# Six gate projections as seven products of half blocks in a hybrid FFT and mLSTM block

## The chip, the cores and the metric

The kernel runs on one core of a Trainium2 chip. A core has TensorE (PE, matrix products), VectorE (DVE), ScalarE (ACT), GpSimdE (POOL) and SyncE (SP), which here only issues transfers; 16 DMA engines move data between DRAM and the core's memory. The metric is device time of one execution in microseconds (us), as the median of several. One more execution is recorded by the hardware profiler; the rows that are quoted come from it.

## The reference

The input is one sequence of 512 tokens with 1024 channels, all in float32. What matters here:

```python
h = rmsnorm(x, norm_w[l])
proj = h @ w_in[l]
x_f, z_f, x_m, z_m, o_m, g_logits = jnp.split(proj, split_points, axis=-1)

y_a = (fourier_mix(x_f) * jax.nn.silu(z_f)) @ w_fourier[l]

x_c = jax.nn.silu(centred_dwconv(x_m, conv_w[l], conv_b[l]))
q = block_diag_proj(x_c, w_q[l])
k = block_diag_proj(x_c, w_k[l])
v = block_diag_proj(x_m, w_v[l])
...                                   # gates i and f of both directions
h_cell = jnp.transpose(h_fwd + h_bwd, (0, 2, 1, 3))
h_cell = h_cell * jax.nn.sigmoid(o_m.astype(jnp.float32)).reshape(bsz, seq, M_HEADS, M_HEAD_DIM)
h_cell = h_cell * lax.rsqrt(jnp.mean(h_cell * h_cell, axis=-1, keepdims=True) + EPS)
h_cell = h_cell.reshape(bsz, seq, M_WIDTH).astype(x.dtype) * hnorm_w[l]
y_b = ((h_cell + skip_w[l] * x_c) * jax.nn.silu(z_m)) @ w_mlstm[l]

g_a, g_b = jnp.split(jax.nn.sigmoid(g_logits), N_BRANCHES, axis=-1)
x = x + (g_a * y_a + g_b * y_b) @ w_out[l]

return rmsnorm(x, final_norm_w)
```

The mLSTM has four heads of 512 channels. `z_m` and `o_m` are the two gates of each head: each is a product of the normalised input (512 x 1024) with 1024 x 512 weights. These gates are what the change touches.

## The kernel before

**Arithmetic.** Every float32 operand is split into a high and a low part, and a product is three matmuls: high x high, high x low, low x high (lines 97 to 99). The high part is a copy on ACT (line 90), the low part a subtraction on DVE (line 93).

**Weights.** All weights come in units of 128 x 1024 floats (512 KB), in the order of one list, `plan`. `fetch` loads a unit on SP's queue into one of three `raw` buffers; `prepare` splits it into `whi` and `wlo`, of which there are two buffers each (a stage late in the kernel, from about 490 us, has two more, `gwh` and `gwl`). `unit()` prepares ahead until two units are there and hands out the first. A unit's split can therefore begin when TensorE has finished with the unit two back. A unit holds 24 matmuls of 512 columns.

**Stages.** The first 20 units or so are projections that feed a convolution on DVE and ACT. Then come the four heads, one after the other; after them the branch's output product, the Fourier branch, the merge and the last product. These later projections and the last product are worked as blocks of 2 x 2 in seven products instead of eight, with sums of weight blocks that are formed in DRAM during the earlier stages: `sum_job` copies 1 MB on SP's queue and, one job later, adds another 1 MB to it in an accumulating transfer on POOL's queue. The table `JOBS` says before which units the jobs come, and one more is placed in each head after q and after the scores.

**One head.** q is projected (`vhi`, `vlo`), then scores `sp` = k x q per token block (TensorE), multiplied on DVE by decay weights `ws` of both directions: for each of four token blocks, 640 columns, because the diagonal block is there once per direction (lines 516 to 528). Meanwhile TensorE does o's four units (lines 557 to 559). DVE adds the weighted scores per direction (`sf`, `sb_`), TensorE sums them over partitions into `den` (line 608); ACT takes the absolute value (612), DVE the maximum (613) and the reciprocal (614), ACT spreads the result over the partitions (618, `rs`, in the tiles phi and plo). DVE multiplies `ws` by it (623 to 625), and `phi` and `plo` are its two parts. TensorE projects v (`vp`, line 636, small matmuls) and forms pv from those parts. z's four units stand around den, pv and the transposes (`z_unit`, evacuated at 367, SiLU at 369). pv is multiplied by the sigmoid of o (572, 652), POOL computes the inverse root of its mean square (`rr`, 656 and 657), DVE scales (658), TensorE transposes (668), and DVE combines skip, norm weight and z (670, 671) into u, which is split again into `sa` and `sb`.

**What sets the order.** The Tile scheduler orders each engine's instructions from dependences, buffers and its own model of durations; some are pinned to the order of the program. Each engine then works through its list in that order, and waits at the first instruction whose inputs or buffer are not ready.

Of the kernel before, what the change touches and what calls it, by code (L numbers as in the profile page):

```python
# [14 lines left out]
S = 512  # L15
# [6 lines left out]
NB = 5  # L22
JOBS = (10, 13, 16, 22, 26, 29, 34, 37, 42, 45, 51, 56, 60)
# [7 lines left out]
LOW = ("ones", "mhalf", "warm", "vecs", "raw", "whi", "wlo", "consts", "rb", "rc", "rr", "ss", "fss", "gb")  # L31
# [9 lines left out]
def hybrid_block(ctx: ExitStack, tc, xT, xn, first, units, blocks, vecs, gates, gbias, consts, dft, fnw, out):  # L41
# [430 lines left out]

    u_hi, u_lo = {}, {}
    for h in range(NH):
# [37 lines left out]
        def decay():  # L512
            ws = [tl(f"wf{b}", [P, 640]) for b in range(4)]
            for dr in range(2):
                bc = bank("acc")
                te.matmul(bc, bsel[:, 4 * dr + h : 4 * dr + h + 1].to_broadcast([P, P]), mx_r, start=True, stop=True)
                for b in range(4):
                    n = (b + 1) * P
                    o, s = (slice(n, 640), slice(b * P, S)) if dr == 0 else (slice(0, n), slice(0, n))
                    r = 32 * dr + h  # L520
                    se.activation(ws[b][:, o], bc[:, s], AF.Exp, scale=-1.0, bias=a_col[:, b, r : r + 1])
            for b in range(4):
                n = (b + 1) * P
                blk = ws[b][:, n : n + P]
# [5 lines left out]
            return ws  # L530

        if h > 0:
            ws = decay()
        sps = []
        for b in range(4):
            sp = bank("wk")
# [7 lines left out]
        else:  # L544
# [3 lines left out]
            ws = decay()  # L548
        ops = [bank("acc") for _ in range(4)]
# [16 lines left out]
        o_unit(0)  # L566
        so2 = [tl(f"so{n}", [P, 2, S]) for n in range(2)]
        so = [so2[t // 2][:, t % 2, :] for t in range(4)]

        def o_gate():  # L570
            for t in range(4):
                se.activation(so[t], ops[t], AF.Sigmoid, scale=rc[:, t : t + 1])
# [7 lines left out]
        for acc, first, rest, off in ((sf, 0, (1, 2, 3), P), (sb_, 3, (2, 1, 0), 0)):  # L580
            for b in rest:
                n = (b + 1) * P
                rng = slice(n - P, S) if off else slice(0, n)
                wr = slice(n, 640) if off else slice(0, n)
                if b == rest[0]:
                    full = slice(P, 640) if off else slice(0, S)
                    keep = slice(0, P) if off else slice(n, S)
                    keepw = slice(P, 2 * P) if off else slice(n, S)
                    ve.tensor_copy(acc[:, keep], ws[first][:, keepw])
                    fr = slice(2 * P, 640) if off else slice(0, n)  # L590
                    ve.tensor_tensor(out=acc[:, rng], in0=ws[first][:, fr], in1=ws[b][:, wr], op=ALU.add)
                else:
# [565 lines left out]
```

## Time and profile before

| | before |
|---|---|
| median of 3 runs | 759.44 us (759.43 to 759.52) |
| profiled execution | 760.22 us |
| its span, first to last instruction | 758.2 us |
| PE busy, matmuls | 747.4 us (99%), 4140 |
| weight loads on PE (PEld) | 642.5 us |
| DVE busy | 527.3 us (70%) |
| ACT busy | 411.1 us (54%) |
| POOL busy | 69.6 us |
| DMA | 128.55 MB, mean 170 GB/s |
| granted TensorE clock | 0.998 |

Times are in us unless marked ns. PE is TensorE's matmul row and PEld its weight loads, which overlap. A row of a group reads: line, engine, operation, output<-inputs, shape, count, then busy time and mean ns of one, then the engine's idle time just before and what ended it. A row of the timeline starts with the start and the duration. Matmuls overlap in the pipeline, so their duration is longer than the distance from one start to the next.

### The profile page before, as it was taken

To read this page: it belongs to the slowest core of one execution; us is meant where nothing else is said; L and a number is where in the kernel's file an instruction comes from. 1 tells how busy PE (TensorE), PEld (TensorE's weight loads), DVE (VectorE), ACT (ScalarE), POOL (GpSimd) and SP (SyncE) were. 2 spreads that over 40 slices of the span, in tenths; PEclk is the share of its full clock that TensorE was granted. 3 is DMA by queue.
4 is the path that set the end of the run, shared out by engine and by line. 5 is a ranking of instruction groups with operands and counts; after the bars stand their busy time and mean duration, and the time that the engine had idled before them with its cause. 6 is when DMAs were issued, how large, how long until landed. Compare 5 with 4: busy or idle time off the path is not lost.

```text
span 758.2 us, 10932 instructions
## 1 busy us (share of the span) xinstructions
PE 747.4 (99%) x4140; PEld 642.5 (85%) x4140; DVE 527.3 (70%) x821; ACT 411.1 (54%) x645; POOL 69.6 (9%) x147
## 2 busy tenths in 40 slices
PE   8999999999999999999999999999999999999996
PEld 7888875888888888888888888899999999988885
DVE  6999983696759475867584856257676787556976
ACT  7345557468447652776362443266544587543444
POOL 0001000104100310041003010000020100000003
PEclk9999999999999999999999999999999999999999
DMA  8538776176924891479214973277655456554452
GB/s 287 181 137 231 206 226 173 35 235 161 217 105 157 215 238 61 170 184 226 108 56 161 225 217 120 84 215 216 189 161 165 113 161 199 170 182 156 136 195 111
DMA packets 40805, 128.55 MB, mean 170 GB/s; under 512 B 4785, under 2 KB 5426, under 8 KB 35634
## 3 DMA queue, kind: packets, MB, share of 16 engines
q1 hardware_dynamic: 36658, 104.14, 40.2%
q0 software_dynamic: 3520, 23.07, 15.0%
q10 hardware_dynamic: 576, 0.66, 0.3%
q8 instruction: 32, 0.52, 0.3%
q14 instruction: 19, 0.16, 0.1%
HBM read 125.76 MB, written 44.04 MB: 224 GB/s over the span
## 4 chain that ended last, share of the span: by engine, by line
PE 96%; DVE 1%; ACT 1%; DMA 1%; POOL 0%; issue 0%; ACTq 0%; POOLq 0%
PE acc L97 17%; PE acc L99 17%; PE acc L98 17%; PE wk L97 8%; PE wk L99 8%; PE wk L98 8%; PE acc L558 3%; PE acc L559 3%; PE acc L557 3%; PE wk L636 2%; PE acc L1008 1%; PE acc L1007 1%; PE acc L1006 1%; PE wk L302 1%; PE wk L668 1%; DMA raw<-in_first_dram 1%
## 5 line engine op out<-in xcount | busy, mean ns | idle before, releaser
L93 DVE TENSOR_TENSOR wlo<-raw,whi 128x1024 fp32r<-128x1024 f32 (+2 forms) x107 | 125.0, 1172 | 80.2 <-ACT whi L90 79.6
L90 ACT ACTIVATE whi<-raw 128x1024 fp32r<-128x1024 f32 (+2 forms) x107 | 108.7, 1019 | 130.6 <-PE acc L98 81.6
L97 PE MATMUL acc<-hhi,whi 128*128 128x512 f32 x240 | 94.2, 392 | 0.0
L98 PE MATMUL acc<-hlo,whi 128*128 128x512 f32 x240 | 93.5, 390 | 0.0
L99 PE MATMUL acc<-hhi,wlo 128*128 128x512 f32 x240 | 93.5, 390 | 0.0
L93 DVE TENSOR_TENSOR gwl<-raw,gwh 128x1024 fp32r<-128x1024 f32 (+1 forms) x39 | 47.1, 1209 | 18.0 <-ACT gwh L90 17.9
L90 ACT ACTIVATE gwh<-raw 128x1024 fp32r<-128x1024 f32 (+1 forms) x39 | 40.9, 1049 | 30.8 <-PE acc L98 11.1
L97 PEld LDWEIGHTS acc<-hhi,whi 128*128 128x128 f32 x240 | 45.1, 188 | 10.0 <-issue 0.8
L99 PEld LDWEIGHTS acc<-hhi,wlo 128*128 128x128 f32 x240 | 45.0, 188 | 9.4
L98 PEld LDWEIGHTS acc<-hlo,whi 128*128 128x128 f32 x240 | 45.1, 188 | 9.1
L559 PE MATMUL acc<-whi,hlo 128*128 128x512 f32 x128 | 50.4, 394 | 0.0
L558 PE MATMUL acc<-wlo,hhi 128*128 128x512 f32 x128 | 50.4, 393 | 0.0
L98 PE MATMUL acc<-sb,whi 128*128 128x512 f32 x128 | 50.1, 391 | 0.0
L98 PE MATMUL wk<-vlo,phi 128*128 128x512 f32 x128 | 49.8, 389 | 0.0
L97 PE MATMUL acc<-sa,whi 128*128 128x512 f32 x128 | 49.8, 389 | 0.0
L97 PE MATMUL wk<-vhi,phi 128*128 128x512 f32 x128 | 49.6, 389 | 0.0
L99 PE MATMUL acc<-sa,wlo 128*128 128x512 f32 x128 | 49.0, 391 | 0.0
L99 PE MATMUL wk<-vhi,plo 128*128 128x512 f32 x128 | 48.0, 389 | 0.0
L557 PE MATMUL acc<-whi,hhi 128*128 128x512 f32 x128 | 47.7, 393 | 0.0
L331 DVE SCALAR_TENSOR_TENSOR t2k<-sa,vecs,t2k 128x511 f32<-128x511 f32 (+1 forms) x64 | 45.2, 744 | 0.1
L93 DVE TENSOR_TENSOR vlo<-wk,vhi 128x512 fp32r<-128x512 f32 x32 | 20.5, 676 | 15.7 <-ACT vhi L90 15.7
L98 PEld LDWEIGHTS acc<-sb,whi 128*128 128x128 f32 x128 | 24.0, 188 | 5.0
(409 smaller groups left out, 1910.7 us busy)
## 6 DMA issues: line engine op xcount, KB each, us to landing
raw<-in_units_dram SPq DMA_DIRECT2D x69, 512.0 KB, 4.1
sum<-in_blocks_dram SPq DMA_DIRECT2D x20, 1024.0 KB, 8.1
raw<-sum SPq DMA_DIRECT2D x64, 256.0 KB, 3.7
raw<-in_blocks_dram SPq DMA_DIRECT2D x48, 256.0 KB, 3.9
sum<-in_blocks_dram POOLq DMA_DIRECT2D x10, 1024.0 KB, 9.3
sum<-sum POOLq DMA_DIRECT2D x10, 1024.0 KB, 8.2
raw<-sum SPq DMA_DIRECT2D x8, 512.0 KB, 4.1
raw<-in_blocks_dram SPq DMA_DIRECT2D x6, 512.0 KB, 4.2
```

The source lines that it names most:

```text
L90: pin(se.activation(dst, src, AF.Copy, scale=scale), pinned)
L93: pin(ve.tensor_tensor(out=dst, in0=src, in1=hi.bitcast(F32), op=ALU.subtract), pinned)
L97: pin(te.matmul(acc, wh, xh, start=start, stop=False, **skip), pinned)
L98: te.matmul(acc, wh, xl, start=False, stop=False, **skip)
L99: te.matmul(acc, wl, xh, start=False, stop=stop, **skip)
L302: pin(te.matmul(gate_ps[rows, :], w_gate[j][:, i, :], r, start=n == 0, stop=n == 14, tile_position=(0, 32 * (2 * b + j))), n + b + j > 0)
L331: ve.scalar_tensor_tensor(out=cv[:, o], in0=src[:, s], scalar=cw[k], in1=cv[:, o], op0=ALU.mult, op1=ALU.add)
L557: te.matmul(ops[t], hv(x_hi, k)[:, ts], wh[:, ks], start=k == 0, stop=False)
L558: te.matmul(ops[t], hv(x_hi, k)[:, ts], wl[:, ks], start=False, stop=False)
L559: te.matmul(ops[t], hv(x_lo, k)[:, ts], wh[:, ks], start=False, stop=k == 7)
L636: te.matmul(vp[:, ds], xm[c0 + d][:, b * P : (b + 1) * P], vbf[:, d, :], start=True, stop=True)
L668: te.transpose(tp[:, t * P : (t + 1) * P], so[t][:, d * P : (d + 1) * P], ident)
```

## The change

In heads 1 to 3 both gates of a head are computed as 2 x 2 blocks: tokens in halves of 256, input channels in halves of 512, output channels in halves of 256. Seven products of such blocks take the place of eight, with four of them on sums of blocks (s1 to s4). Each product is one weight unit of 24 matmuls of 256 columns (line 554), so a gate has seven units where it had four. Head 0 stays as it was.

- The sums of x blocks are made once (`x_sums`, `split_t2`, `split_t3`); x is loaded again for them, eight loads of 256 KB.
- The sums of the weight blocks are 12 more copies and accumulations in DRAM; `JOBS` and `ORDER` put those of the heads first.
- The products end in three PSUM banks per gate (X, Y, Z) and are combined with copies on ACT and additions on DVE, in halves.
- The decay weights have 512 columns and a separate tile `dg` for the second copy of the diagonal block.
- The hi and lo split of head 0's u is done in head 3.

```diff
-NB = 5
-JOBS = (10, 13, 16, 22, 26, 29, 34, 37, 42, 45, 51, 56, 60)
+NB = 8
+ORDER = (5, 6, 7, 0, 1, 2, 3, 4)
+SEVEN = ("a11", "s1", "a12", "s2", "s4", "s3", "a22")
+N0, NHEAD, NYB = 24, 14, 16
+JOBS = (6, 8, 10, 12, 14, 16, 18, 20, 22, 27, 33, 41, 47, 55, 61, 67, 70, 73, 76, 79, 85, 92, 99, 106, 113)
...
-    plan = [[units[i]] for i in range(64)] + [seq[i : i + 2] for i in range(0, len(seq), 2)]
+    plan = [[units[i]] for i in range(N0)]
+    for h in range(1, NH):
+        for kind in range(2):
+            for name in SEVEN:
+                src = sums[4 + h, int(name[1]) - 1] if name[0] == "s" else blocks[4 + h, {"a11": 0, "a12": 1, "a22": 3}[name]]
+                plan.append([src[:, 1024 * kind : 1024 * kind + 1024]])
+    plan += [[units[i]] for i in range(N0, N0 + NYB)]
...
+    def x_sums():
+        hi, lo = (tl(t, [P, 4, 256], F32R) for t in ("rawx", "t0l"))
+        for j in range(2):
...
+            for n in range(2):
+                k = 2 * j + n
+                xr = [tl(f"{t}{k}", [P, S]) for t in ("vhi", "vlo")]
+                for a in range(2):
+                    nc.sync.dma_start(xr[a], xT[k + 4 * a])
+                    se.activation(xr[a], xr[a], AF.Copy, scale=col(V_NW + k + 4 * a))
...
+                ve.tensor_tensor(out=r0[:, n], in0=b11, in1=b12, op=ALU.subtract)
+                ve.tensor_tensor(out=r2[:, k], in0=b22, in1=b12, op=ALU.subtract)
+                ve.scalar_tensor_tensor(out=r1[:, n], in0=r0[:, n], scalar=-1.0, in1=b22, op0=ALU.mult, op1=ALU.subtract)
+                ve.scalar_tensor_tensor(out=r3[:, k], in0=r1[:, n], scalar=-1.0, in1=b21, op0=ALU.mult, op1=ALU.subtract)
+            hi_of(hi[:, js], r0)
+            lo_of(lo[:, js], r0, hi[:, js])
...
+        def product(key, xs, first):
+            if first:
+                b[key] = bank("acc").rearrange("p (m c) -> p m c", m=2)
+            acc = b[key]
+            w = [v.rearrange("p (k c) -> p k c", k=4) for v in unit()]
+            for m in range(2):
+                ms = slice(m * P, (m + 1) * P)
+                for k in range(4):
+                    for n, (iw, ix) in enumerate(((0, 0), (0, 1), (1, 0))):
+                        wk, xk = w[iw][:, k], xs[k][ix]
+                        l, r = (xk[:, ms], wk) if tokens_out else (wk[:, ms], xk)
+                        te.matmul(acc[:, m], l, r, start=first and m == 0 and k == 0 and n == 0, stop=k == 3 and n == 2, skip_group_check=True)
+            return acc
+
+        def a11():
+            se.activation(dst(0, 0), product("X", x_blk(0, 0), True), AF.Copy)
+
+        def s1():
+            se.activation(dst(1, 1), product("Z", t_sums[0], True), AF.Copy)
+
+        def a12():
+            ve.tensor_tensor(out=dst(0, 0), in0=product("Y", x_blk(1, 0), True), in1=dst(0, 0), op=ALU.add)
+
+        def s2():
+            se.activation(dst(0, 1), product("X", t_sums[1], False), AF.Copy)
+
+        def s4():
+            ve.tensor_tensor(out=dst(0, 1), in0=product("Z", x_blk(1, 1), False), in1=dst(0, 1), op=ALU.add)
+            if last:
+                last(0)
...
-            ws = [tl(f"wf{b}", [P, 640]) for b in range(4)]
+            ws = [tl(f"wf{b}", [P, S]) for b in range(4)]
+            dg = tl("dg", [P, 4, P])
...
+        ve.tensor_tensor(out=dgf, in0=rs[0], in1=dgf, op=ALU.mult)
         for b in range(4):
             n = (b + 1) * P
-            ve.tensor_tensor(out=ws[b][:, n:640], in0=rs[0][:, n - P : S], in1=ws[b][:, n:640], op=ALU.mult)
             ve.tensor_tensor(out=ws[b][:, 0:n], in0=rs[1][:, 0:n], in1=ws[b][:, 0:n], op=ALU.mult)
-            ve.tensor_tensor(out=ws[b][:, n - P : n], in0=ws[b][:, n - P : n], in1=ws[b][:, n : n + P], op=ALU.add)
...
-        if h > 0:
-            z_unit(0)
+            new_sz()
+            step_z = seven_z()
+            step_z.pop(0)()
+            step_z.pop(0)()
         ss = tl("ss", [P, 4], bufs=2)
         for t in range(4):
             pv = bank("wk")
...
+            if h > 0:
+                step_z.pop(0)()
+        if h == 3:
...
+                u_hi[c], u_lo[c] = tl(f"sa{c}", [P, S], F32R), tl(f"sb{c}", [P, S], F32R)
+                hi_of(u_hi[c], uu)
+                lo_of(u_lo[c], uu, u_hi[c])
```

The order of the instructions changes at three places of interest. Rows name the line, the operation and output<-inputs; numbers behind a name tell one tile from the next of the same name.

DVE in head 2, from den's maximum on, before; `vlo` are v's lo parts, `wlo_2845` the lo part of a z unit:

```order
L613 TENSOR_TENSOR t2k_2559<-t2k_2559,phi_497_2540 128x512
L93 TENSOR_TENSOR vlo_521_2636<-wk_2630,vhi_520_2635 128x512
L614 RECIPROCAL t2k_2559<-t2k_2559 128x512
L93 TENSOR_TENSOR vlo_524_2645<-wk_2639,vhi_523_2644 128x512
L367 TENSOR_TENSOR sz_531_2691<-acc_2816,rb_240 128x512
L93 TENSOR_TENSOR wlo_2845<-raw_2699,whi_2844 128x1024
L93 TENSOR_TENSOR vlo_527_2654<-wk_2648,vhi_526_2653 128x512
```

And now, where `wlo_3103`, `wlo_3156` and `wlo_3207` belong to the units a12, s2 and s4 of z, and `acc_3154` is a12's product:

```order
L96 TENSOR_TENSOR wlo_3103<-raw_3034,whi_3102 128x1024
L96 TENSOR_TENSOR vlo_557_3000<-wk_2994,vhi_556_2999 128x512
L758 TENSOR_TENSOR t2k_2894<-t2k_2894,phi_530_2875 128x512
L759 RECIPROCAL t2k_2894<-t2k_2894 128x512
L96 TENSOR_TENSOR vlo_560_3009<-wk_3003,vhi_559_3008 128x512
L96 TENSOR_TENSOR vlo_563_3018<-wk_3012,vhi_562_3017 128x512
L96 TENSOR_TENSOR wlo_3156<-raw_3072,whi_3155 128x1024
L96 TENSOR_TENSOR vlo_566_3027<-wk_3021,vhi_565_3026 128x512
L564 TENSOR_TENSOR sz_570_3065<-acc_3154,sz_570_3065 128x2x256
L771 TENSOR_TENSOR dg_2648<-phi_539_2898,dg_2648 128x512
```

Seven multiplies of `wf` by the reciprocal (lines 776 and 774) follow, and then `wlo_3207`. One unit's split stood behind the reciprocal and ahead of those multiplies before; now it is s2's, with s4's right behind them.

DVE at the turn from head 2 to head 3, before; `wlo_3183` and `wlo_3306` belong to coming units, lines 670 and 671 make u:

```order
L670 SCALAR_TENSOR_TENSOR t2k_2941<-wk_2936,vecs_108,sb_124_689 128x512
L671 TENSOR_TENSOR t2k_2917<-t2k_2917,sz_531_2691 128x512
L671 TENSOR_TENSOR t2k_2929<-t2k_2929,sz_531_2691 128x512
L671 TENSOR_TENSOR t2k_2941<-t2k_2941,sz_532_2692 128x512
L93 TENSOR_TENSOR sb_565_2921<-t2k_2917,sa_564_2920 128x512
L93 TENSOR_TENSOR wlo_3183<-raw_3104,whi_3182 128x1024
```

And now, where `wlo_3542` and `wlo_3602` belong to s1 and a12 of the next head's o gate, and line 601 evacuates a22 of z:

```order
L601 SCALAR_TENSOR_TENSOR sz_571_3066<-acc_3067,rb_252 128x2x256
L841 SCALAR_TENSOR_TENSOR t2k_3383<-wk_3378,vecs_120,sb_110_621 128x512
L841 SCALAR_TENSOR_TENSOR t2k_3395<-wk_3390,vecs_120,sb_117_664 128x512
L841 SCALAR_TENSOR_TENSOR t2k_3407<-wk_3402,vecs_120,sb_124_705 128x512
L96 TENSOR_TENSOR wlo_3542<-raw_3314,whi_3541 128x1024
L842 TENSOR_TENSOR t2k_3383<-t2k_3383,sz_570_3065 128x512
L842 TENSOR_TENSOR t2k_3395<-t2k_3395,sz_570_3065 128x512
L842 TENSOR_TENSOR t2k_3407<-t2k_3407,sz_571_3066 128x512
L96 TENSOR_TENSOR wlo_3602<-raw_3349,whi_3601 128x1024
```

A unit's split now stands behind every three operations on u, where it stood behind seven before.

SP's queue during the first projections, now; `vhi_201` to `vlo_208` are the loads for the x sums (line 497), and `sum_96` is a weight sum's copy:

```order
L142 DMA raw_414<-in_units_dram 128x1024
L171 DMA sum_96<-in_blocks_dram 128x2048
L497 DMA vhi_201_1117<-in_xT_dram 128x512
L497 DMA vlo_202_1118<-in_xT_dram 128x512
L497 DMA vhi_203_1127<-in_xT_dram 128x512
L497 DMA vlo_204_1128<-in_xT_dram 128x512
L497 DMA vhi_209_1151<-in_xT_dram 128x512
L497 DMA vhi_207_1141<-in_xT_dram 128x512
L497 DMA vlo_208_1142<-in_xT_dram 128x512
L142 DMA raw_461<-in_units_dram 128x1024
```

Before, the raw loads followed each other there, with the first copy for a weight sum four raw loads later.

More of the change, by code (lines that the diff above doesn't have):

```diff
@@ L30 @@
 SUMS_AT = ((0, 3), (0, 5), (1, 1), (1, 3))
-LOW = ("ones", "mhalf", "warm", "vecs", "raw", "whi", "wlo", "consts", "rb", "rc", "rr", "ss", "fss", "gb")
+LOW = ("ones", "mhalf", "warm", "vecs", "raw", "whi", "wlo", "consts", "rb", "rc", "rr", "ss", "gb")
 HIGH = ("sz0", "sz1", "so0", "so1", "t2k")
@@ new lines, in x_blk, with seven, s3, a22 @@
+    def x_blk(a, t):
+        return [tuple(hv(v, k + 4 * a)[:, 256 * t : 256 * t + 256] for v in (x_hi, x_lo)) for k in range(4)]
+    def seven(tokens_out, dst, last):
+        b = {}
+        def product(key, xs, first):
[23 more added lines that the diff above has]
+                last(0)
+        def s3():
+            X = product("X", t_sums[2], False)
+            ve.scalar_tensor_tensor(out=dst(1, 1), in0=X, scalar=-1.0, in1=dst(1, 1), op0=ALU.mult, op1=ALU.subtract)
+        def a22():
+            X = product("X", t_sums[3], False)
+            if last:
+                last(1, X)
+            else:
+                se.activation(dst(1, 0), X, AF.Copy, scale=-1.0)
+        return [a11, s1, a12, s2, s4, s3, a22]
@@ L547, in hybrid_block @@
             gate_cols(rows)
-            ws = decay()
-        ops = [bank("acc") for _ in range(4)]
+            ws, dg = decay()
+            ops = [bank("acc") for _ in range(4)]
         def o_part(n, w, pieces):
@@ L564, in o_unit @@
             o_part(n, unit(), PIECES)
-        o_unit(0)
-        so2 = [tl(f"so{n}", [P, 2, S]) for n in range(2)]
+        if h == 0:
+            o_unit(0)
+            so2 = [tl(f"so{n}", [P, 2, S]) for n in range(2)]
+        else:
+            steps.pop(0)()
         so = [so2[t // 2][:, t % 2, :] for t in range(4)]
@@ L579, in hybrid_block @@
+            ve.tensor_tensor(out=dg[:, b], in0=sps[b][:, n - P : n], in1=dg[:, b], op=ALU.mult)
         sf, sb_ = t2k(), t2k()
[L580 to L592, printed above, removed]
-                    ve.tensor_tensor(out=acc[:, rng], in0=acc[:, rng], in1=ws[b][:, wr], op=ALU.add)
@@ L594, in hybrid_block @@
-        o_unit(1)
-        early = 3 if h == 0 else 0
-        w2 = unit()
-        o_part(2, w2, PIECES[:early])
+        ve.tensor_copy(sf[:, 0:P], dg[:, 0])
+        ve.tensor_tensor(out=sf[:, P:S], in0=dg[:, 1:4].rearrange("p b c -> p (b c)"), in1=ws[0][:, P:S], op=ALU.add)
+        for b in (1, 2):
+            o = slice((b + 1) * P, S)
+            ve.tensor_tensor(out=sf[:, o], in0=sf[:, o], in1=ws[b][:, o], op=ALU.add)
+        ve.tensor_copy(sb_[:, 3 * P : S], ws[3][:, 3 * P : S])
+        ve.tensor_tensor(out=sb_[:, 0 : 3 * P], in0=ws[3][:, 0 : 3 * P], in1=ws[2][:, 0 : 3 * P], op=ALU.add)
@@ L598, in hybrid_block @@
+        for b in (1, 0):
+            o = slice(0, (b + 1) * P)
+            ve.tensor_tensor(out=sb_[:, o], in0=sb_[:, o], in1=ws[b][:, o], op=ALU.add)
+        if h == 0:
+            o_unit(1)
+            w2 = unit()
+            o_part(2, w2, PIECES[:3])
+        else:
+            steps.pop(0)()
+            steps.pop(0)()
         em, bc, den = tl("phi2", [P, S]), bank("wk"), bank("wk")
```

142 lines of the change are left out of this document (111 added, 31 removed).

## The prediction

> **What bounds the kernel now.** I read the page's busy shares first, then its slices and its chain of waits, then single stages.
>
> ```profile
> span 758.2 us, 10932 instructions
> PE 747.4 (99%) x4140; PEld 642.5 (85%) x4140; DVE 527.3 (70%) x821; ACT 411.1 (54%) x645; POOL 69.6 (9%) x147
> PE   8999999999999999999999999999999999999996
> PEclk9999999999999999999999999999999999999999
> PE 96%; DVE 1%; ACT 1%; DMA 1%; POOL 0%; issue 0%; ACTq 0%; POOLq 0%
> ```
>
> TensorE is 96% of the chain and fills every slice between the first and the last. So a matmul less is worth its step from start to start, as long as whatever feeds TensorE keeps up. The windows show how near the feeders are to that limit: 60:80 lies in the first projections, 220:240 and 300:320 around two heads' middle, 500:520 in a stage that works with 256 columns already.
>
> ```profile
> 60.00:80.00 20.00, 20.00 (x90) 16.57 (x89) 18.98 (x26) 10.19 (x14) 0.83 (x1) 1.00 0.88 230
> 220.00:240.00 20.00, 20.00 (x106) 17.11 (x105) 16.46 (x29) 13.61 (x19) 0.00 (x0) 1.00 0.09 29
> 300.00:320.00 20.00, 20.00 (x106) 17.09 (x105) 16.10 (x25) 14.97 (x22) 0.00 (x0) 1.00 0.35 124
> 500.00:520.00 20.00, 20.00 (x174) 20.00 (x173) 13.43 (x18) 13.71 (x21) 0.00 (x0) 1.00 0.74 223
> ```
>
> The columns after the window are busy time of PE, weight loads, DVE, ACT and POOL. TensorE never waits here, but around a head's middle DVE is busy for 16 of 20 us and ACT for 14 to 15. In 500:520 the 256-column products run without a gap; that stage has four buffers for split weights (whi, wlo, gwh, gwl), the heads only two.
>
> **What it removes from TensorE.** Heads 1 to 3 lose 6 gates x 96 = 576 matmuls of 512 columns and get 6 x 7 x 24 = 1008 of 256. The steps:
>
> ```profile
> 235.63 0.39 PE L98 MATMUL acc<-hlo,whi 128*128 128x512 f32 x1
> 239.71 0.39 PE L98 MATMUL acc<-hlo,whi 128*128 128x512 f32 x1
> 659.78 0.28 PE L99 MATMUL wk<-th,wlo 128*128 128x256 f32 x1
> 661.18 0.28 PE L99 MATMUL wk<-bh,wlo 128*128 128x256 f32 x1
> ```
>
> 18 steps lie between the first two: 0.227 us each. 12 lie between the others: 0.1167. So 576 x 0.227 = 130.7 becomes 1008 x 0.1167 = 117.6: **-13.1 us**. The whole 500:520 window would give 20.00/174 = 0.115, and -14.8; it holds some smaller matmuls, so I take -13.1.
>
> **What it does to the feeding.** A unit of weights needs ACT's hi split, then DVE's lo split, and neither may start before TensorE has left the buffer two units back:
>
> ```profile
> L93 DVE TENSOR_TENSOR wlo<-raw,whi 128x1024 fp32r<-128x1024 f32 x100 | 122.0, 1222 | 76.6 <-ACT whi L90 76.0 <-PE wk L99 0.5
> L90 ACT ACTIVATE whi<-raw 128x1024 fp32r<-128x1024 f32 x100 | 105.8, 1060 | 126.1 <-PE acc L98 81.6 <-issue 20.3 <-PE wk L98 6.2
> ```
>
> DVE's wait before wlo is for ACT, ACT's before whi for a matmul: the chain is 1.06 + 1.22 and some 0.1 for two hand-overs, 2.4 us. TensorE covers it with the unit between: 24 x 0.227 = 5.45 us now, 24 x 0.1167 = 2.80 after. The slack falls from 3.0 to 0.4 us, while the units of a head go from 8 to 14. Six more units cost DVE 6 x 1.13 (its step) = 6.8 us a head and ACT 6 x 1.06 = 6.4. The seven products' combining adds three DVE operations (1.9 us) to an output gate and some 1.3 us to a z gate, and seven ACT copies of 0.6 (4.2 us). In the sum DVE still fits: about 59 us of steps in a head of 75. In order it does not, because DVE and ACT take their work one by one, and the largest piece stands between den and the pv products:
>
> ```profile
> 226.45 0.48 PE L608 MATMUL wk<-vlo,half_r 128*128 128x512 f32 x1
> 245.42 0.39 PE L97 MATMUL wk<-vhi,phi 128*128 128x512 f32 x1
> 226.96 0.60 ACT L612 ACTIVATE t2k<-wk 128x512 f32<-128x512 f32 x1
> 232.18 1.28 ACT L618 ACTIVATE phi<-t2k 64x512 f32<-64x512 f32 x2
> 233.48 1.27 ACT L618 ACTIVATE plo<-t2k 64x512 f32<-64x512 f32 x2
> 227.59 0.69 DVE L613 TENSOR_TENSOR t2k<-t2k,phi 128x512 f32<-128x512 f32 x1 [1.26 <-ACT t2k L612]
> 228.80 3.34 DVE L614 RECIPROCAL t2k<-t2k 128x512 f32<-128x512 f32 x1
> 233.80 1.69 DVE L623 TENSOR_TENSOR wf<-phi,wf 128x512 f32<-128x512 f32 x4
> 236.00 1.68 DVE L624 TENSOR_TENSOR wf<-plo,wf 128x128 f32<-128x128 f32 x4
> 237.61 1.22 DVE L93 TENSOR_TENSOR wlo<-raw,whi 128x1024 fp32r<-128x1024 f32 x1
> 241.74 3.03 DVE L93 TENSOR_TENSOR plo<-wf,phi 128x640 fp32r<-128x640 f32 x4
> ```
>
> From D, the start of den's last matmul, to pv TensorE now has 19 us of work in this head, three units of it z weights. In the new order it has 11.2 (12 small vp matmuls 1.3, 79 matmuls of 256 columns 9.2, three of 512 0.7). DVE's own chain (max, reciprocal, eight multiplies, lo splits) is no shorter.
>
> **The walk of head 2's middle**, in the new order with these durations; times after D. TensorE needs s2's wlo at D + 5.4 (vp 1.3, 31 products 3.6, and two of 512 columns). ACT's abs starts at D + 0.5, DVE's max at 1.1, the reciprocal runs from 1.75 to 5.0 (a step of 3.26), two vlo splits of 0.6 follow, and s2's wlo runs from 6.2 to 7.4: TensorE waits **2.0**. s2 then ends at 10.0. Behind s2's wlo stand in DVE's queue one vlo 0.6, the evacuation of a12 0.6, the multiply of dg 0.6 and seven of wf (0.2 to 0.6 each, 2.6 in all), and only then s4's wlo: it starts at 11.8 and is done at 13.0. TensorE wants it at 10.7, after two products of s4, two of s3 and the bc matmul: **2.3** more. If DVE comes late to the max, the first wait grows: the a12 weights' hi split stands on ACT behind a sigmoid table load and two sigmoids,
>
> ```profile
> L572 ACT ACTIVATE so<-acc,rc 128x512 f32<-128x512 f32 x16 | 10.3, 695 | 1.0 <-PE acc L559 0.9
> L572 ACT ACT_TABLE_LOAD x4 | 5.1, 1283 | 0.1
> ```
>
> 1.3 + 1.3 us there, which puts a12's wlo at about D + 2 and the max behind it, at D + 3.2; s2's wlo then ends at 9.5, 3.5 after TensorE asks for it (its own wait of 0.6 at a12 included). The three heads have nearly the same order here: 4.3 to 5.5 us each, I take 4.9, **+14.7** for three. What is late next, pv's plo, no longer is: TensorE gets to pv at D + 15.6, when the first plo is done by 15.5.
>
> **The turn from one head to the next.** After the last z products DVE does, at 0.6 to 0.75 each,
>
> ```profile
> L670 DVE SCALAR_TENSOR_TENSOR t2k<-wk,vecs,sb 128x512 f32<-128x512 f32 x16 | 11.4, 745 | 6.2 <-PE wk L668 6.2
> L671 DVE TENSOR_TENSOR t2k<-t2k,sz 128x512 f32<-128x512 f32 x16 | 10.4, 682 | 0.0
> L93 DVE TENSOR_TENSOR sb<-t2k,sa 128x512 fp32r<-128x512 f32 x16 | 10.5, 684 | 0.2
> ```
>
> four of each, 7.4 us, between the lo splits of the next head's o units. Counted from the end of z's s3: the evacuation of a22 cannot start before 4.1, three operations of line 670's kind follow to 7.0, o's s1 wlo is done at 8.3 and wanted at 7.5 (0.8); three of line 671's kind and a wlo come out level; three lo splits and one more of 670's kind put s2's wlo at 14.8 against 14.0 (0.8); together 2 when ACT is on time, up to 4 when the 1.1-us SiLU and the hi splits are late as well. I take 3 for each of the two turns between these heads and 1.1 for the turn out of head 0, whose z gate is as before: **+7.1**.
>
> **The x sums and the rest.** Seven of eight loads of 256 KB stand on SP's queue ahead of a raw weight load; 16 DVE operations of 256 columns (0.34 each, 5.4 us) and their splits come in where DVE is busy 18.98 of 20. Bounds 0 (the wlo there are early by about 2 us) and +3; **+1**. The decay weights change DVE by under 1 us a head and ACT by three small exponentials; their cover is gone in the middle, but they stand elsewhere in the order: 0. Head 3's 12 moved hi and lo pieces for head 0's u lie beside pv: 0, bound +1. Twelve more weight sums, each a copy of 1 MB and an accumulation, move 24 MB more:
>
> ```profile
> raw<-in_units_dram SPq DMA_DIRECT2D x69, 512.0 KB, 4.1
> sum<-in_blocks_dram SPq DMA_DIRECT2D x20, 1024.0 KB, 8.1
> sum<-sum POOLq DMA_DIRECT2D x10, 1024.0 KB, 8.2
> L657 POOL TENSOR_TENSOR rr<-rr,mhalf 128x1 f32<-128x1 f32 x16 | 9.5, 595 | 1.3
> ```
>
> A unit now wants 512 KB each 2.80 us, 187 GB/s, below the 223 of window 500:520. Bounds 0 and +6, when an accumulation on POOL's queue waits for a copy (8.1 us) and the rr of head 2's last tokens, and so the transposes, stand behind it; I take 0.
>
> **Sum.** Against the profiled execution, 760.22 (span 758.2 and 2.0 around it): -13.1 + 14.7 + 7.1 + 1 = +9.7, so 769.9. The median of the runs shown is 0.8 lower, 759.44: **769 us**.
>
> **Rivals.** (A) The forecast: stalls of 16 to 29 us, 762 to 775 us. (B) The feed holds, in the heads' middles above all: DVE and ACT run so far ahead that a wlo is never last. Its place is line 96 behind line 759, its gain the whole 13.1, 746 us at no stall; it decides faster as long as the stalls stay under 11.6 us in all, that is under 2.6 in each middle and little at the turns. For it speak the DVE share of 70% and window 500:520, where units of this length run without a gap; against it the two buffers and the 3.3-us reciprocal in the same queue. (C) The stalls eat just the gain, 11.6 to 14.6 us: 759.4. (D) The transfers: one POOL wait of 6 and raw loads late behind copies early on, 3, atop A: 778. (E) The clock falls. A stall long enough to halve it would cost the unit behind it another 2.80; one such in each middle and turn, six, gives 769 + 17 = 786. Against it:
>
> ```profile
> 8.52 0.50 PE L97 MATMUL wk<-hhi,whi 128*128 128x512 f32 x1 [2.10 <-ACT whi L90]
> 4.00:10.00 6.00, 3.90 (x23) 3.19 (x23) 2.42 (x5) 2.96 (x7) 0.00 (x0) 1.00 1.00 348
> ```
>
> an idle time of 2.1 us passed with the clock at 1.00, and the longest single stall of my walk is 3.5. The Trainium skill ("TensorE: Matmul & The Clock Gate", section "HAM oscillation — how this bites in real kernels") gives the rule that TensorE should have no idle gaps above some 3.4 us, or its clock is halved. By that rule only the late case of my first wait would be near it; the row of 2.1 us agrees, and no longer one is here.
>
> **Chances.** A 0.64, B 0.21, C 0.07, D 0.06, E 0.02. Measurements of this kernel tell about 0.2% (1.5 us) from no change. So slower 0.72 (A, D, E), within 0.07 (C), faster 0.21 (B). The range reaches into B as far as half its stalls, 752, and above D's middle, 780: 752 to 780; A's own is 762 to 775.
>
> **What would show it.** Matmul steps of the gates at 0.117 (else the -13.1 is wrong). TensorE no longer 20.00 of 20, with idle time before lines 554 put down to DVE's wlo of line 96, 4 to 5 us between a head's den and its pv, most at s2 and s4, and 2 to 4 us at the turns. Granted clock still 1.00. My forecast is wrong if TensorE's idle time in heads 1 to 3 is under 12 us, or if the waits end with DMA (raw) or POOL (rr) rather than with splits.

## The result: 6.5% slower, and the profile after

The changed kernel takes 809.62 us (805.88 to 810.94), the kernel before 759.43: a ratio of 1.0654, 95% interval 1.0622 to 1.0687. That is 50 us more, where I had forecast 10. The page of the changed kernel: its span, busy shares, slices and chain.

```profile
span 804.1 us, 12039 instructions
PE 760.6 (95%) x4572; PEld 668.0 (83%) x4572; DVE 566.0 (70%) x882; ACT 446.7 (56%) x707; POOL 79.3 (10%) x159
PE   8999979999999969889999999999999999999996
PEclk9999999999999988998999999999999999999999
PE 65%; DVE 12%; DMA 10%; ACT 9%; issue 3%; POOL 0%; SPq 0%; ACTq 0%; POOLq 0%; DVEq 0%
```

TensorE has holes in the sixth slice and most in the fifteenth, where the clock falls as well. Its share of the chain goes from 96% to 65%. DVE (12%) and ACT (9%) are of the kind that I had expected; DMA has 10%, where it had 1%. Two stages show it (the columns are those of the windows before):

```profile
100.00:120.00 20.00, 15.29 (x59) 11.59 (x57) 15.79 (x27) 10.22 (x14) 1.62 (x2) 0.91 1.03 317
280.00:300.00 20.00, 13.43 (x82) 11.91 (x82) 8.44 (x13) 4.53 (x8) 1.85 (x2) 0.90 1.02 251
```

In both the 16 DMA engines are full (1.03, 1.02) and TensorE is idle for 5 to 7 of 20 us. In the second DVE and ACT have little to do either (8.44 and 4.53 of 20 us): nobody has weights. In the first DVE has the convolution and the x sums (15.79), but stands still for 4.22 us before the late unit's lo split. The chain's pieces (start, duration, what) name the transfers:

```profile
82.95 20.05 DMA raw<-in_units_dram
280.03 20.23 DMA raw<-sum
300.34 1.07 ACT whi L93
301.43 1.24 DVE wlo L96
```

Two raw loads of 512 KB took 20 us each, where the medians of their groups are 4.7 and 4.5. What was issued around the second, on SP's queue and on POOL's:

```profile
266.21 0.50 SPq L171 DMA_DIRECT2D sum<-in_blocks_dram  x1
271.68 0.50 SPq L171 DMA_DIRECT2D sum<-in_blocks_dram  x1
276.09 0.50 SPq L171 DMA_DIRECT2D sum<-in_blocks_dram  x1
280.03 0.32 SPq L142 DMA_DIRECT2D raw<-sum  x1
```

```profile
272.24 0.88 POOL L175 DMA_DIRECT2D sum<-in_blocks_dram  x1
273.89 0.82 POOL L175 DMA_DIRECT2D sum<-sum  x1 [0.77 <-DMA sum<-in_blocks_dram]
281.01 0.81 POOL L175 DMA_DIRECT2D sum<-in_blocks_dram  x1 [6.30 <-DMA sum<-in_blocks_dram]
```

Three copies and three accumulations of 1 MB stand within 15 us around the raw load. From 278 to 302 us the accumulations (q0, POOL's queue) and everything on SP's queue (q1) moved about the same number of bytes, but the accumulations took nearly twice the time of the 16 engines (packets, MB, share of the 16 engines):

```profile
q0 software_dynamic: 416, 3.01, 65.2%
q1 hardware_dynamic: 694, 3.05, 35.6%
```

To split the 46 us that the span grew by, I took each distance from one matmul's start to the next: the step of its width (0.227, 0.117 or 0.11 us) counts as work, up to as much again as clock where the trace shows the half clock, and what is left as waiting. Work falls from 730.5 to 719.1 us, waiting rises from 19.2 to 64.4, and the half clock costs 12.0: -11.4 + 45.2 + 12.0 = 45.8. About 3 us of this waiting are no waiting: the gates' 1008 matmuls come every 0.12 us (see below), and the split counts 0.117. The same split for the runs below:

| run | median, us | work | waiting | half clock |
|---|---|---|---|---|
| before | 759.4 | 730.5 | 19.2 | 0.0 |
| changed | 809.6 | 719.1 | 64.4 | 12.0 |
| no weight sums | 778.5 | 718.7 | 46.8 | 4.1 |
| copies, no accumulations | 779.1 | 718.7 | 47.4 | 3.1 |
| before, with the new sums | 768.9 | 730.1 | 26.5 | 1.3 |
| no sums, no reciprocal | 772.5 | 718.6 | 43.1 | 2.5 |
| no sums of any kind | 773.8 | 718.4 | 42.9 | 3.1 |
| decay weights and u's move | 765.5 | 731.2 | 23.7 | 0.0 |

### The profile page after: what moved, and what is told of

Its sections match the earlier page's. It is cut to its first block, busy times and chain, and to the rows that moved or that the text cites. A ratio compares the mean times of both kernels' runs of the same rounds, so it can differ in the third digit from the quotient of the medians.

```text
span 804.1 us, 12039 instructions
## 1 busy us (share of the span) xinstructions
PE 760.6 (95%) x4572; PEld 668.0 (83%) x4572; DVE 566.0 (70%) x882; ACT 446.7 (56%) x707; POOL 79.3 (10%) x159
## 3 DMA queue, kind: packets, MB, share of 16 engines
q1 hardware_dynamic: 42130, 128.26, 46.6%
q0 software_dynamic: 5248, 35.65, 22.2%
## 4 chain that ended last, share of the span: by engine, by line
PE 65%; DVE 12%; DMA 10%; ACT 9%; issue 3%; POOL 0%; SPq 0%; ACTq 0%; POOLq 0%; DVEq 0%
PE acc L100 11%; PE acc L101 11%; PE acc L102 11%; PE acc L554 8%; PE wk L100 5%; PE wk L102 5%; PE wk L101 5%; DMA raw<-sum 5%; DVE wlo L96 4%; DMA raw<-in_units_dram 2%; DMA raw<-in_blocks_dram 2%; ACT whi L93 2%; PE wk L314 1%; PE acc L1180 1%; PE acc L1178 1%
## 5 line engine op out<-in xcount | busy, mean ns | idle before, releaser
L96 DVE TENSOR_TENSOR wlo<-raw,whi 128x1024 fp32r<-128x1024 f32 (+2 forms) x125 | 147.1, 1179 | 104.8 <-ACT whi L93 103.9
L93 ACT ACTIVATE whi<-raw 128x1024 fp32r<-128x1024 f32 (+2 forms) x125 | 127.7, 1024 | 153.2 <-PE acc L101 50.7
L100 PE MATMUL acc<-hhi,whi 128*128 128x512 f32 x144 | 56.9, 395 | 1.7 <-ACT whi L93 1.7
L102 PE MATMUL acc<-hhi,wlo 128*128 128x512 f32 x144 | 56.9, 395 | 0.5 <-DVE wlo L96 0.5
L101 PE MATMUL acc<-hlo,whi 128*128 128x512 f32 x144 | 56.6, 393 | 0.0
L343 DVE SCALAR_TENSOR_TENSOR t2k<-sa,vecs,t2k 128x510 f32<-128x510 f32 (+1 forms) x64 | 44.8, 746 | 0.0
L554 PE MATMUL acc<-whi,hhi 128*128 128x256 f32 x96 | 27.8, 290 | 4.1 <-ACT whi L93 3.2
L554 PE MATMUL acc<-hhi,whi 128*128 128x256 f32 x96 | 29.1, 304 | 2.2 <-ACT whi L93 1.6
L554 PE MATMUL acc<-hhi,wlo 128*128 128x256 f32 x96 | 29.3, 306 | 1.7 <-DVE wlo L96 1.7
L554 PE MATMUL acc<-hlo,whi 128*128 128x256 f32 x96 | 28.9, 301 | 0.0
L100 PEld LDWEIGHTS wk<-vhi,phi 128*128 128x128 f32 x128 | 24.2, 189 | 4.7
```

The costliest lines, as they stand in the source:

```text
L93: pin(se.activation(dst, src, AF.Copy, scale=scale), pinned)
L96: pin(ve.tensor_tensor(out=dst, in0=src, in1=hi.bitcast(F32), op=ALU.subtract), pinned)
L100: pin(te.matmul(acc, wh, xh, start=start, stop=False, **skip), pinned)
L101: te.matmul(acc, wh, xl, start=False, stop=False, **skip)
L102: te.matmul(acc, wl, xh, start=False, stop=stop, **skip)
L343: ve.scalar_tensor_tensor(out=cv[:, o], in0=src[:, s], scalar=cw[k], in1=cv[:, o], op0=ALU.mult, op1=ALU.add)
```

## The experiments

### All weight sums left out

```diff
-    sums = {(b, k): dram.tile([P, 4 * S], F32, tag=f"sum{b}{k}", name=f"sum{b}{k}") for b in range(NB) for k in range(4)}
+    sums = {(b, k): blocks[b, k] for b in range(NB) for k in range(4)}
...
-        if state["job"] <= 4 * NB:
+        if state["job"] < 0:
```

What was read as a sum is one block of it here.

> Leaves out all 32 weight sums (copies and accumulations); where a sum was read, the unsummed weight block is read. Theory T (transfers: raw weight loads come late behind the 1 MB copies and accumulations, and the waits halve the clock): the long waits at 102, 286 and 296 us and the half-clock stretches go, and what is left is the order's waits in the heads: 755 to 768 us. Rival F (feeding: two buffers of split weights and the in-order queues of ACT and DVE): the idle time of TensorE in the heads stays at 30 us or more with the half clock: 790 to 805 us.

Measured: 778.49 us, ratio 1.0234 (1.0162 to 1.0306). It lies between the two: 31 us of the 50 hang on the sums, 19 do not. (The two profiled executions lie 26 apart, 17.6 of waiting and 7.9 of clock in the table.) The page and the waits of TensorE (us in total, times, longest):

```profile
PE 749.6 (96%) x4572; PEld 660.6 (85%) x4572; DVE 566.4 (73%) x882; ACT 446.6 (57%) x707; POOL 53.6 (7%) x127
PE acc L554 <- DVE wlo L96: 5.1, 9, 0.9
PE acc L554 <- ACT whi L93: 3.1, 4, 0.8
PE wk L314 <- ACT sb L345: 2.0, 1, 2.0
```

No wait at line 554 is longer than 1.3 us here; in the changed kernel the second of these rows is

```profile
PE acc L554 <- ACT whi L93: 10.4, 6, 4.8
```

and its longest wait, 4.8 us, is the one behind the raw load of 20 us.

### The new sums alone, and the old sums alone

The 12 new sums left out, with the 20 old ones at their old places by position in the heads:

```diff
-NB = 8
-ORDER = (5, 6, 7, 0, 1, 2, 3, 4)
+NB = 5
+ORDER = (0, 1, 2, 3, 4)
+JOBS = (10, 13, 16, 22, 27, 33, 41, 47, 55, 61, 69, 74, 78)
...
```

> Leaves out the 12 new weight sums of heads 1 to 3 (their units are read from unsummed blocks) and sets the 20 old ones at the places they had, by position in the heads. T: as without any sums, at most 6 us above it: 758 to 772 us. F: 790 to 805 us.

The kernel before, with the new sums formed and not used:

```diff
-NB = 5
-JOBS = (10, 13, 16, 22, 26, 29, 34, 37, 42, 45, 51, 56, 60)
+NB = 8
+ORDER = (5, 6, 7, 0, 1, 2, 3, 4)
+JOBS = (6, 8, 10, 12, 14, 16, 18, 20, 22, 26, 29, 34, 37, 42, 45, 49, 52, 55, 58, 61, 67, 74, 81, 88, 95)
...
```

> The kernel before with the 12 new weight sums formed as well (nothing reads them), and with the changed kernel's table of jobs by position. T: raw loads late in the first projections here too, where a unit still takes 5.45 us; TensorE idle 5 to 12 us there and a half-clock stretch or two: 765 to 780 us. F: hidden, 759 to 761 us.

Measured: 798.83 us (ratio 1.0501, 1.0436 to 1.0567) and 768.87 us (1.0108, 1.0046 to 1.0169). The first lies where F had it, but not for F's reason. With the old traffic alone, TensorE still waits 3.3 and 4.0 us in head 2's o gate, from 280 and 292 us, with raw loads of up to 23.5 us. So 11 us go with the new sums, and 20 with the old ones. In the kernel before, whose units last 5.45 us in the heads, raw loads took up to 11.3 us and TensorE had no wait for them. The second lies in T's range, though not at the place I had named: the first projections keep TensorE busy throughout, and the waits stand in the Fourier stage from 508 to 562 us, whose units are short, behind raw loads of 6 to 10 us on the chain. Both fit one account: the sums cost where units are short.

### Copies or accumulations

```diff
-        if i > 0:
+        if i < 0:
             b, k = ORDER[(i - 1) // 4], (i - 1) % 4
```

> The changed kernel with its 32 copies of 1 MB on SP's queue where they are, and the accumulations on POOL's queue left out (what is read as a sum is a copy of one block). If the accumulations crowd the raw loads: 777 to 785 us, raw loads landing in 5 us again. If the copies do, ahead of the raw loads in SP's queue: 795 to 808 us.

Measured: 779.10 us, ratio 1.0262 (1.0233 to 1.0292), the same as without any sums. First the queues there (packets, MB, share of 16 engines' span), with the median us from issue to landing of the copies and raw loads; then the same of the changed kernel, with the accumulations from `blocks`:

```profile
q1 hardware_dynamic: 42130, 128.26, 49.6%
q0 software_dynamic: 640, 2.10, 0.9%
sum<-in_blocks_dram SPq DMA_DIRECT2D x32, 1024.0 KB, 7.8
raw<-in_units_dram SPq DMA_DIRECT2D x45, 512.0 KB, 4.0
```

```profile
q1 hardware_dynamic: 42130, 128.26, 46.6%
q0 software_dynamic: 5248, 35.65, 22.2%
raw<-in_units_dram SPq DMA_DIRECT2D x45, 512.0 KB, 4.7
sum<-in_blocks_dram POOLq DMA_DIRECT2D x16, 1024.0 KB, 12.0
```

The 32 copies stand in SP's queue as before, and cost nothing that shows (0.6 us against the run without any sums). The 32 accumulations are the 30 us. They move 33.6 MB (35.65 - 2.10) and take 21.3% (22.2 - 0.9) of 16 engines in 804 us, 5.4 us of all 16 each; SP's queue moves 128 MB in 46.6%. Per MB an accumulation holds the engines 1.7 times as long. Against plain copies of the same 1 MB it is 1.9 times: in the run with the copies on ACT's queue (next section) the copies take 11.3% of the engines' span (11.5 - 0.2), the accumulations 21.5% (22.4 - 0.9). POOL's queue as such is not what makes it long: what else it moves (2.10 MB, 0.9%) takes 1.1 times as long per MB as SP's queue. The raw loads follow: the longest takes 6.1 us without sums, 11.6 with the copies alone and 20.2 in the changed kernel.

### Where the jobs stand, and on which queue the copies go

Copies issued from ACT (`nc.sync` to `nc.scalar` in `sum_job`); jobs spread; and both:

```diff
+JOBS = (6, 10, 14, 18, 21, 23, 27, 32, 36, 41, 46, 50, 55, 60, 64, 67, 70, 72, 75, 78, 81, 85, 92, 99, 106, 113, 120, 127)
...
             sps.append(sp)
-        next_job()
+        if h == 0:
+            next_job()
```

> The changed kernel with the 32 copies for the weight sums issued from ACT instead of SP, so that a raw load no longer stands behind a copy in SP's queue. T with the queue as the cause: 770 to 785 us. T with the DMA engines' throughput as the cause: 800 to 812 us, raw loads still 10 to 20 us late at the same places. F: 803 to 812 us.

> Same work, the 33 jobs of the weight sums spread: one each four units in the first projections instead of one each two, one after q and three in each of heads 1 to 3 about 19 us apart, the last seven in the Fourier stage. Theory T (transfers crowd the raw loads where jobs stand close together): the waits at 102 and 286 to 302 us and their half-clock stretches go, 782 to 795 us, near the 778.5 without any jobs. Rival B (the DMA engines are short of throughput as a whole, wherever the jobs stand): 800 to 812 us.

> Same work, jobs spread and their copies issued from ACT. Theory T with two causes (jobs too close together, and a raw load behind a copy in one queue): the gains add, 780 to 787 us. If both cure the same waits: 793 to 800 us.

Measured: 799.35 (ratio 1.0508, 1.0451 to 1.0565), 795.63 (1.0478, 1.0428 to 1.0528) and 806.44 us (1.0624, 1.0589 to 1.0659). The first and the second lie just outside the ranges, 10 and 14 us faster than the changed kernel, and the third lies above both of its own: the gains do not add. With both, head 2 waits 4.5 us before s3 again, and the Fourier stage waits more than with either. The longest raw load falls from 20.2 us to 14.6, 13.1 and 11.8, but the median of all rises from 4.4 to 4.8, 4.8 and 5.3. So neither the order in SP's queue nor the spacing alone is the cause; the run without accumulations names it. I take it that it matters where a given table puts the accumulations against the raw loads, which is not shown, and I have no table that hides them all.

### More room for the split weights

Two buffers of 1024 columns cut into four of 512, with the products taken by channel block:

```diff
-            for m in range(2):
-                ms = slice(m * P, (m + 1) * P)
-                for k in range(4):
+            for k in range(4):
+                for m in range(2):
+                    ms = slice(m * P, (m + 1) * P)
...
+        for a in range(0, w, S):
+            hi.append(tl("gwh" if extra else "whi", [P, S], F32R, bufs=4))
+            lo.append(tl("gwl" if extra else "wlo", [P, S], F32R, bufs=4))
```

> Same work, the two buffers of 1024 columns for split weights cut into four of 512, and a product takes its weights by channel blocks, so that the first half is free again half way through. Theory F (the 26 us of waits left without jobs come from the buffer two units back): a split may start 4.2 us before its use instead of 2.8, waits in the heads fall from 20 to under 10 us: 785 to 798 us. Rival Q (they come from what stands ahead in ACT's and DVE's queues, the reciprocal, sigmoids and combining): 803 to 815 us, as splits in two pieces also cost ACT and DVE 0.1 us more a unit.

> Both the half buffers and the spread jobs. T and F: the gains add, 760 to 778 us. Q and B: 795 to 812 us.

Without jobs and x sums, and then with a third hi buffer in the room (`bufs=3` for `whi`):

> No weight sums and no sums of x blocks (the products read x blocks instead). The x sums make the convolution end late (2.1 us and a half-clock stretch): 770 to 774 us against 778.5. If another order takes the gain back: 776 to 780 us.

> As the run without jobs and x sums, with a third buffer for the hi parts of weights in the room of the x sums, so that ACT's split need not wait for the unit two back. Theory F (the buffer): 4 to 10 us faster than that run, waits of the seven products on whi gone. Theory Q (the queues' order): within 3 us of it, or slower.

Measured: 822.65 (ratio 1.0834, 1.0782 to 1.0885), 822.51 (1.0832, 1.0741 to 1.0923), 773.83 (1.0195, 1.0154 to 1.0236) and 787.88 us (1.038, 1.0336 to 1.0424). More room made it slower every time: by 13 us with half buffers and by 27 with spread jobs, both beyond what Q had expected, and by 14 with the third buffer, which Q allowed. Most of the short waits for wlo go, but longer ones come: with half buffers 7.3 us at the convolution's end (3.2 in the changed kernel), with the third buffer 4.2 us for an evacuation of z on DVE, with half buffers and spread jobs 5.9 us for the scaling of pv. For this last one DVE waits for POOL's `rr`, and that stands behind an accumulation that waits for its copy:

```profile
367.58 0.81 POOL L186 DMA_DIRECT2D sum<-sum  x1 [9.87 <-DMA sum<-in_blocks_dram]
369.33 0.49 DVE L838 TENSOR_SCALAR so<-so,rr 128x512 f32<-128x512 f32 x1 [8.70 <-POOL rr L837]
```

For the others I take it that the scheduler puts splits further ahead in the queues of ACT and DVE, and other work comes late behind them; that is not shown. Nor is it shown that the buffer two units back limits: what would happen with a third buffer and the same order was not tried. The run without x sums is 4.7 us faster than the one without jobs, as expected, but the intervals of the two ratios overlap, so the cost of the x sums is known only roughly.

### The reciprocal

```diff
-        ve.reciprocal(out=r, in_=r)
+        ve.tensor_copy(r, r)
```

> No weight sums (as in the run without jobs, 778.5 us) and the four reciprocals replaced by a copy of the same tile on DVE, which leaves out the division. Theory Q (what stands ahead of a split in the queues of DVE and ACT sets the waits of the heads, and between den and pv it is the 3.3-us reciprocal): the waits behind line 759 in the middle of each head, 2.3 to 3.9 us and a half-clock stretch, go; 764 to 771 us. If the reciprocal is only one of many and others take its place: 773 to 779 us.

Measured: 772.52 us (ratio 1.0176, 1.0103 to 1.0249), between the two ranges. The middle of head 2 goes from 2.9 us of waits to 1.5, of head 3 from 3.3 to 1.6; head 1's stays (2.3 and 2.4). The half-clock stretch of head 2 goes, and one in head 3 comes. The scheduler also orders differently with the shorter instruction, so these 6 us are not the reciprocal's alone.

### The x sums at another place

```diff
-    x_sums()
-
...
             gate_cols(rows)
             ws, dg = decay()
+            x_sums()
```

> Same work, the sums of x blocks (8 loads, 16 DVE operations and their splits) made in head 0 after its decay weights instead of ahead of the heads. If they are what makes the convolution late (the wait of 3.35 us at 117 us and the half clock behind it): 798 to 806 us. If that wait comes from the raw load that is 20 us late at 103 us: 805 to 812 us.

Measured: 805.55 us (ratio 1.0608, 1.0496 to 1.0721), in both ranges, so the time does not choose between them. The convolution ends without its wait, and head 0 waits 9 us more than in the changed kernel: the cost moves with them.

### Parts of the change alone

Only the o gates, only the z gates, and neither, with a flag for each kind in `plan` and in the heads, such as

```diff
+        o7, z7 = O7 and h > 0, Z7 and h > 0
-        if h > 0:
+        if o7:
             steps, so2 = seven_o()
```

> Only the o gates of heads 1 to 3 in seven products, with half of the new weight sums; the z gates as before (they read a block of x that the sums have overwritten, so their values are left out of account). Half the gain of TensorE (-6 us). Q: the middle keeps a z feed of 5.45 us a unit, waits only at the turns and before den, and in the first projections by the jobs: 762 to 775 us. Theory T: jobs still crowd the first projections but the heads' units come slower: 765 to 775 us. If each gate costs the same: 782 to 788 us.

> Only the z gates of heads 1 to 3 in seven products, with half of the new weight sums; the o gates as before (they read a block of x that the sums have overwritten). Q: the middle of each head keeps its waits (3 to 4 us each and some half clock): 775 to 790 us, slower than with the o gates alone. If each gate costs the same: 782 to 788 us.

> The kernel before with only the decay weights of 512 columns and head 0's u split in head 3; all gates, sums and jobs as before. My prediction's step priced both at 0 to +1: 758.5 to 761 us. If they move the scheduler's order in the heads: up to 765 us.

And the decay weights with head 0's u split where it was:

> The kernel before with only the decay weights of 512 columns; head 0's u split where it was. If the move of u's split into head 3 costs the 7 us (waits of 1.4 and 1.9 us behind head 3's pv): 758 to 761 us. If the decay weights do: 764 to 766 us.

Measured: 796.65 (ratio 1.0494, 1.0444 to 1.0544), 788.35 (1.0385, 1.0241 to 1.0528), 765.49 (1.0084, 1.0051 to 1.0116) and 762.09 us (1.0033, 1.0017 to 1.0049). The o gates alone lie above all ranges given, and the z gates alone in Q's. By the medians the o gates are the slower ones, against what I expected, but the intervals overlap, as the two times with the z gates are 8.9 us apart. I take it that both being so slow is the accumulations again, since both keep all 32 (12 of them half as long): after the heads both have some 10 us more waiting than the kernel before. That is not shown. What I had priced at nothing costs 6 to 7 us: 2.4 for the decay weights, 3.4 and more for u's move. The waits of TensorE with both:

```profile
PE acc L101 <- ACT sa L94: 1.7, 1, 1.7
PE wk L849 <- DVE so L827: 1.3, 1, 1.3
```

and ACT behind head 3's pv, where lines 834 and 94 are the eight moved operations:

```profile
409.18 1.65 ACT L834 ACTIVATE t2k<-sb 128x512 f32<-128x512 f32 x3
410.74 1.66 ACT L94 ACTIVATE sa<-t2k 128x512 fp32r<-128x512 f32 x3
412.30 0.62 ACT L834 ACTIVATE t2k<-sb 128x512 f32<-128x512 f32 x1
412.95 0.63 ACT L94 ACTIVATE sa<-t2k 128x512 fp32r<-128x512 f32 x1
```

They stand beside no pv at all but after its squares, 4.4 us in all. The output product needs their `sa`: its first matmul starts at 411.40, when the first of them is done.

### What halves the clock

Matmuls of no use, of 256 columns, put ahead of o's s4 (12) and s3 (24) in head 2; the scheduler placed 30 before s4 and 6 before s3:

```diff
+        def fill(n):
+            if h == 2 and tokens_out:
+                for _ in range(n):
+                    te.matmul(b["Y"][:, 0], hv(x_hi, 0)[:, 0:P], hv(x_hi, 0)[:, 0:256], start=True, stop=True, skip_group_check=True)
```

> The changed kernel with 36 more matmuls of 256 columns in head 2's o gate, written to a bank whose content has been used: 30 of them (3.5 us) just before s4, where TensorE waited at 286 us, 6 before s3, where it waited at 296 us. If the half clock follows from an idle TensorE: the stretch at 289 us goes, the one behind the wait before s3 stays; time 0 to 3 us less than the changed kernel's, though 4.2 us of work are added. If the half clock comes from something else (load, temperature, the transfers): the stretch at 289 us stays, and the time is 2 to 4 us more.

Measured: 815.79 us (ratio 1.0746, 1.0713 to 1.0778), 6 us above the changed kernel and beyond both forecasts, and a half-clock stretch at 288 us all the same. The fillers ran before 286 us, the wait for weights went on for another 2.7 us behind them, and the stretch of 3.41 us from 284.9 was 32% busy. So the run did not fill the hole, and it decides nothing by itself. What decides is the clock in all traces together. Windows of the changed kernel, cut at the clock's own steps of 3.41 us (PE's busy time is the second number, the clock the third from the end):

```profile
285.95:289.36 3.41, 0.80 (x5) 0.39 (x3) 0.95 (x2) 1.98 (x4) 0.00 (x0) 1.00 1.03 274
289.36:292.77 3.41, 3.27 (x8) 2.60 (x9) 1.54 (x3) 0.60 (x2) 0.00 (x0) 0.50 1.04 298
422.50:425.90 3.40, 1.60 (x11) 1.40 (x12) 3.40 (x7) 2.02 (x4) 0.00 (x0) 1.00 0.08 12
425.90:429.30 3.40, 3.40 (x17) 3.30 (x17) 3.40 (x8) 1.81 (x4) 0.00 (x0) 0.50 0.81 261
```

A window in which TensorE did little is followed by one at half clock; in the second pair no single wait was longer than 1.44 us. (A row counts each matmul with its whole duration. With a matmul counted as long as its step, the two windows at full clock are 11% and 35% busy.) Over the 20 profiles of this case, counted by steps: of the windows at full clock, all 72 that were under 39.5% busy were followed by half the clock, none of the 4359 above 42.5% were, and 4 of 8 in between. This is observed, not brought about by an experiment.

## Why the prediction was wrong, step by step

**TensorE's gain, -13.1: too large by 3.4.** The new matmuls' step is 0.12 us, not 0.1167 (18 steps between these rows), so 1008 of them take 121.0 us and the gain is 9.7.

```profile
271.73 0.28 PE L554 MATMUL acc<-hhi,wlo 128*128 128x256 f32 x1
273.89 0.28 PE L554 MATMUL acc<-whi,hlo 128*128 128x256 f32 x1
```

**The heads' middles, +14.7: the mechanism was right for most of it, the size too high.** The last den matmul of head 2 starts at 327.86 us, D:

```profile
329.90 3.35 DVE L759 RECIPROCAL t2k<-t2k 128x512 f32<-128x512 f32 x1
334.31 1.22 DVE L96 TENSOR_TENSOR wlo<-raw,whi 128x1024 fp32r<-128x1024 f32 x1
339.85 1.22 DVE L96 TENSOR_TENSOR wlo<-raw,whi 128x1024 fp32r<-128x1024 f32 x1
```

D + 2.0, 6.5 and 12.0, where my walk had 1.75, 6.2 and 11.8. But TensorE asked later. I had counted 12 small vp matmuls at 1.3 us; each is two records in the trace and they take 2.7 us. It waits 0.9 for s2, 1.2 for s3 and 0.8 for s4: 2.9 us, not 4.9. In the three heads, as far as line 554's waits without sums go, it is 2.3, 2.9 and 3.3, in all 8.5. The waits for s2 and s4 are for wlo, as I had walked. The one for s3 is not: s3 adds to the bank of s2's product, and ACT's copy out of it (line 567) stands behind the hi split of s3's own weights. s3 starts at 340.00:

```profile
338.40 1.06 ACT L93 ACTIVATE whi<-raw 128x1024 fp32r<-128x1024 f32 x1 [1.45 <-PE acc L554]
339.37 0.58 ACT L567 ACTIVATE sz<-acc 128x512 f32<-128x512 f32 x1
```

**The turns, +7.1: about right.** Without sums, waits of over 0.35 us at the three turns are 2.1, 3.3 and 1.1 us, where I had 1.1, 3 and 3. All waits over 0.35 us from head 0's den to head 3's end, without sums, make 21 us, beside 21.8 in my sum, though not at the places I had given each.

**The x sums, +1, and the decay weights and u, 0: undersized.** They measure roughly 4.7, 2.4 and 3.4. I took "beside pv" from the program; in the order, the eight operations on ACT stand behind pv's squares.

**The transfers, bounds 0 to +6, taken as 0: this step failed.** They cost 30; without them the changed kernel's 778.5 lies in my range. I had worked with bandwidth: 187 GB/s wanted, 223 seen. The rows that I had quoted myself, 8.1 us to landing for a copy and 8.2 for an accumulation, I read only as what POOL waits for. What an accumulation does is hold the 16 engines, 5.4 us each, and raw loads of 512 KB then take up to 20 us, three units of 2.8 us ahead being only 8.4. The old 20 sums are part of this: I counted only the new ones, and a cover that was 5.45 us a unit was gone for the old ones as well. The wait on POOL, for which I had put the +6, happens once, in head 2: an accumulation waits 2.31 us for its copy ahead of `rr`, and TensorE waits 1.9 us for the scaling behind it.

```profile
358.11 0.90 POOL L175 DMA_DIRECT2D sum<-sum  x1 [2.31 <-DMA sum<-in_blocks_dram]
359.94 0.49 DVE L819 TENSOR_SCALAR so<-so,rr 128x512 f32<-128x512 f32 x1 [1.22 <-POOL rr L818]
```

Rival D, with 9 us and a chance of 0.06, came nearest: it had raw loads late and this POOL wait. But it had the loads late behind copies, which cost nothing that shows, and not through the accumulations.

**The clock, rival E, chance 0.02: it happened, with less.** I had asked for a single stall long enough, and took the 2.1 us at the kernel's start as a sign that it takes more. The trace's windows show that it takes a window less than about 40% busy, whatever the waits in it: 12 us of the loss. The Trainium skill ("TensorE: Matmul & The Clock Gate", section "HAM oscillation — how this bites in real kernels") speaks of idle gaps of more than 3.4 us. Here waits of 1.44 and 0.81 us in one window were enough, so the measurement decides against reading it as one single gap.

The signs by which I wanted to be judged: the clock is not 1.00, and the longest waits end, through ACT's hi split, with DMA, as I had written for "wrong". The sign "waits of line 554 for wlo" is there too, 5.3 us.

## What to carry to other kernels

When units of work get shorter, every background transfer has to be priced again, the ones that did not show before included: by the share of the DMA engines that its kind takes and not by its bytes, and against the lead of the loads it competes with. Count waits by the window that the clock looks at: several short ones close together cost the wait and then half of the next 3.41 us. And a step that is moved beside other work in the program must be looked up in the order, where it may stand behind it.

## What the runs showed of the hardware

- An accumulating transfer of 1 MB in DRAM held the 16 DMA engines for about 5.4 us (21.3% of 804 us for 32), 1.7 times as long per MB as SP's loads and copies and 1.9 times as long as a plain copy of 1 MB (21.5% and 11.3% for 32 of each); leaving 32 out gained 30.5 us, leaving the 32 copies out as well another 0.6.
- The granted clock was halved for 3.41 us or a multiple behind each window of 3.41 us in which TensorE, each matmul counted as long as its step, was under 39.5% busy (72 of 72), and never above 42.5% (0 of 4359).
- A float32 matmul of 128 columns that is not split into parts is two records of 0.11 us each.
